# Moving the down-weight sums from the gate stage to the branch products, on GpSimd's queue

## The chip, the core and the metric

The kernel runs on one NeuronCore of a Trainium2 chip. The metric is the device time of one execution in microseconds. Engines are named as the profile names them: PE (TensorE), DVE (VectorE), ACT (ScalarE), POOL (GpSimd) and SP (SyncE), which here only issues DMAs.

## The reference

One layer of a streaming encoder on 1024 tokens of width 1024, all in float32. The input is normalized and projected; three mixers follow (latent attention "MLA", forgetting attention "fox", a Mamba-2 scan "SSD"), each with its own output weight; a sigmoid gate merges them; then comes a gated MLP with a causal convolution.

```
u = rms_norm(x, norm_mix_g) @ w_in              # u_mla, u_fox, u_ssm, u_gate
y_a, y_b, y_c = mla(u_mla) @ w_br_mla, fox(u_fox) @ w_br_fox, ssm(u_ssm) @ w_br_ssm
g = sigmoid(u_gate + b_gate)
x = x + (g0 * y_a + g1 * y_b + g2 * y_c) @ w_out
a = causal_dwconv(rms_norm(x, norm_ffn_g) @ ffn_w_up, ffn_conv_w, ffn_conv_b)
out = x + (silu(gate(a)) * val(a)) @ ffn_w_down
```

## The kernel before

Every large product is made of three float32r products (high by high, high by low, low by high), so an operand is first split: ACT copies the high part, DVE subtracts it for the low part (`split`, L133 and L134). A 128x512 product with eight blocks of the inner dimension is 24 matmuls.

The stages, in order:

- **Start (0 to about 92 us).** The tokens are normalized and the MLA input projections made. `columns` loads small constants as rows, transposes them on PE into columns (L292, L300) and copies them out on ACT. Its row tile `pr` has one buffer for three users: `pr_g`, and two `pr_f` of two DMAs each (L298).
- **MLA heads and fox values (to 206).**
- **fx (206 to 397).** Four weight blocks of 512 columns (`which` = 3, 0, 1, 4) times eight token tiles `t`, so 32 units, in a written-out order on PE, DVE and ACT. In each unit a few side jobs are placed. `split512` splits one quarter of the next block's weights. `gate_sums` is a generator of which one step runs per unit: the softplus terms, cumulative sums by matmuls with triangular matrices, the transposes `tp` of the fox sums in two halves with their split into `Fh` and `Fl`, then three matmuls into `pd`, their exponentials, a fourth matmul with `trim` into the same bank, and last the transpose of `cum`. `turned` transposes the queries or keys of an earlier unit into a `tp` bank (L699), of which there are two. `down_sums(k)` prepares a Strassen-like scheme for the last stage: from rows k and k+11 of the down weight it makes four 128x512 differences.
- **Attention (397 to about 895),** both kinds, with the conv and gate projections (`mm`, L860) as filling work on PE. GpSimd scales the softmax rows (`pm`, L977).
- **SSD scan (to about 1105),** with the rest of the filling work. PE, DVE and ACT follow a written-out order, planned with costs and due times.
- **Branch products (1119 to 1293).** For each branch b in the order fox (1), MLA (0), SSD (2) the input is loaded and split, and for each of eight output blocks j the weight block is loaded, the gate `gl` is loaded into one of the four `t4` buffers, two products `ybr` are made, DVE multiplies by the gate (L1326), and the sum is added to `mg`: on GpSimd for MLA (L1329), on DVE for SSD (L1331).
- **Output product, second norm, up projection (to 1824), down projection (to the end).** The down projection has seven steps of eleven blocks; steps P5, P6, P7 and P4 read the differences from the buffer `wsum_d` in device memory.

In fx `down_sums` uses the four shared `t4` buffers; SP issues two loads of 512 KB and two stores of 512 KB for each k, with the loads pinned to program order, and GpSimd makes four subtractions of 128x512.

Where no order is written out (SP and GpSimd everywhere, all engines in the branch products), the Tile framework chooses the order of each queue when the program is built. An engine then works through its queue in order; an instruction waits for what it reads and for its buffer.

Of the kernel before, what the change touches and what calls it, by code (L numbers as in the profile page):

```python
# [11 lines left out]
F32 = mybir.dt.float32  # L12
# [9 lines left out]
P = 128  # L22
# [12 lines left out]
NFH = NFF // 2  # L35
# [7 lines left out]
def block_kernel(ctx: ExitStack, tc: tile.TileContext, x, positions, norm_mix_g, w_in, b_gate,  # L43
# [5 lines left out]
    V, A, G, T, SY = nc.vector, nc.scalar, nc.gpsimd, nc.tensor, nc.sync  # L49
# [76 lines left out]
    def uid(s):  # L126
        cnt[0] += 1
        return f"{s}_{cnt[0]}"

    def split(h, l, src, he=None, le=None):  # L130
        he = he or A
        le = le or V
        i = A.activation(h, src, AF.Copy) if he is A else he.tensor_copy(h, src)  # L133
        return i, le.tensor_sub(l, src, f32(h))  # L134
# [27 lines left out]
    def alloc_hn():  # L162
        h = [hp.tile([P, NK, 512], F32R, name=uid("hnh"), tag=f"hnh{i}") for i in range(2)]
        l = [hp.tile([P, NK, 512], F32R, name=uid("hnl"), tag=f"hnl{i}") for i in range(2)]
        return h, l
# [118 lines left out]

    def columns(rp):

        pr = rp.tile([84, P], F32, name="pr_g", tag="pr", bufs=1)
        SY.dma_start(pr[0:24, :], b_gate.rearrange("o (r p) -> (o r) p", p=P))
        SY.dma_start(pr[24:72, :], ssm_conv_w.rearrange("o k (r p) -> (o k r) p", p=P))
        SY.dma_start(pr[72:84, :], ssm_conv_b.rearrange("o (r p) -> (o r) p", p=P))  # L290
        pt = psp.tile([P, 84], F32, name="pcp", tag="tp", bufs=2)
        T.transpose(pt, pr, ident[0:84, 0:84])  # L292
        A.activation(pc_g, pt, AF.Copy, scale=0.5)
        for dst, srcs in ((pc_f1, (ffn_conv_w[:, 0, :], ffn_conv_w[:, 1, :])),
                          (pc_f2, (ffn_conv_w[:, 2, :], ffn_conv_b))):
            pr = rp.tile([88, P], F32, name=uid("pr_f"), tag="pr", bufs=1)
            for i, s in enumerate(srcs):
                SY.dma_start(pr[44 * i:44 * i + 44, :], s.rearrange("o (r p) -> (o r) p", p=P))  # L298
            pt = psp.tile([P, 88], F32, name=uid("pcp"), tag="tp", bufs=2)
            T.transpose(pt, pr, ident[0:88, 0:88])  # L300
            A.activation(dst, pt, AF.Copy)
        pr = rp.tile([NK, P], F32, name="pr_n", tag="prn", bufs=1)
        SY.dma_start(pr, ssm_norm_g.rearrange("o (r p) -> (o r) p", p=P))
        pt = psp.tile([P, NK], F32, name="pcn", tag="tp", bufs=2)
        T.transpose(pt, pr, ident[0:NK, 0:NK])
        A.activation(pc_n, pt, AF.Copy)
        for col, src, sc in ((gq_col, mla_q_gain, 96.0 ** -0.5), (gk_col, mla_k_gain, 1.0)):
            V.memset(col, 1.0)
            SY.dma_start(col[0:64, :], src[0, 0:64].rearrange("(p o) -> p o", o=1))
            if sc != 1.0:  # L310
                V.tensor_scalar_mul(col, col, sc)
        for col, src, sc in ((fq_col, fox_q_gain, 0.125), (fk_col, fox_k_gain, 1.0)):
            SY.dma_start(col[0:64, :], src[0].rearrange("(p o) -> p o", o=1))
            SY.dma_start(col[64:128, :], src[0].rearrange("(p o) -> p o", o=1))
            if sc != 1.0:
                V.tensor_scalar_mul(col, col, sc)
# [282 lines left out]
    def gate_sums():  # L599
# [43 lines left out]
        for g in range(2):  # L643
            pt = tps([8, 4, P])
            for j in range(4):
                T.transpose(pt[:, j, :], F[:, 4 * g + j, :], ident)
            split(Fh[:, 512 * g:512 * g + 512], Fl[:, 512 * g:512 * g + 512], pt.rearrange("p j s -> p (j s)"))
        neg = fp.tile([8, P], F32, name="neg", tag="neg")
        V.memset(neg, -1.0)
        for r in range(4):  # L650
# [8 lines left out]
        T.matmul(pd[:, 0:128], tri, dv, start=True, stop=True)  # L659
        T.matmul(pd[:, 128:256], strict, dv, start=True, stop=True)  # L660
        T.matmul(pd[:, 256:384], ones, dv, start=True, stop=True)
        for i, dst in enumerate((ea, dend, cdec)):
            A.activation(dst.rearrange("p t h -> p (t h)"), pd[:, 128 * i:128 * i + 128], AF.Exp)
        V.tensor_mul(dend, dend, dt)

        T.matmul(pd[:, 384:512], trim, dv, start=True, stop=True)
        cum = ft("cum", (P, P))
        V.tensor_copy(cum, pd[:, 384:512])
        yield
# [6 lines left out]


    with px:
        def down_sums(k):

            w1, w2, s12, s34 = (fpl.tile([P, 2, 512], F32, name=uid("ws"), tag="t4", bufs=4) for _ in range(4))
            for w, r in ((w1, k), (w2, k + NFH)):
                tc.keep_in_program_order(SY.dma_start(
                    w, ffn_w_down[0, r * P:r * P + P, :].rearrange("p (b c) -> p b c", b=2)))
            G.tensor_sub(s12[:, 0, :], w1[:, 1, :], w1[:, 0, :])
            G.tensor_sub(s34[:, 0, :], w2[:, 1, :], w1[:, 1, :])
            G.tensor_sub(s12[:, 1, :], w2[:, 1, :], s12[:, 0, :])
            G.tensor_sub(s34[:, 1, :], w2[:, 0, :], s12[:, 1, :])
            SY.dma_start(wsum_d[k, :, 0:2, :], s12)
            SY.dma_start(wsum_d[k, :, 2:4, :], s34)  # L690

        units = 0
        gs = gate_sums()
        waiting = []
# [16 lines left out]
        with tc.manual_schedule(engines={mybir.EngineType.PE, mybir.EngineType.DVE, mybir.EngineType.Activation}):  # L711
            for i, which in enumerate((3, 0, 1, 4)):
                wh, wl = (lambda k, w=w5[i], j=j: w[k - k % 2][:, j, k % 2, :] for j in range(2))
                for t in range(NT):
                    if which != 4 and t == 0:
                        load512({3: C_FQ, 0: C_FQ + 512, 1: C_Z + 512}[which])
                    if which != 4 and t % 2:
                        split512()
                    if units % 5 in (1, 3) and units // 5 * 2 + units % 5 // 2 < NFH:
                        down_sums(units // 5 * 2 + units % 5 // 2)  # L720
                    p = acc("fx", "mv" if units % 3 == 2 else "mm")
                    units += 1
                    mm3(p, tok(hnh, t), tok(hnl, t), wh, wl, NK)
# [28 lines left out]
    def load_w(pool, src, nk=NK, he=None, le=None):  # L752
        raw = pool.tile([P, nk, P], F32, name=uid("wr"), tag="wr")
        SY.dma_start(raw, src)
        h = pool.tile([P, nk, P], F32R, name=uid("wh"), tag="wh")
        l = pool.tile([P, nk, P], F32R, name=uid("wl"), tag="wl")
        split(h, l, raw, he, le)
        return h, l
# [532 lines left out]
    with ExitStack() as pe_:  # L1291
# [5 lines left out]
            pass  # L1297
        run_until(clk[0] + 100.0)
        mh, ml = alloc_hn()
        for b, wsrc, nk in ((1, w_br_fox, 4), (0, w_br_mla, 4), (2, w_br_ssm, 8)):  # L1300
            ah, al = [], []
            for k in range(nk):
# [12 lines left out]
            wv = wsrc[0].rearrange("(k p) c -> p k c", p=P)  # L1315
            for j in range(NK):
                wh, wl = load_w(fpl, wv[:, :, j * P:j * P + P], nk)
                g = fpl.tile([P, S], F32, name=uid("gl"), tag="t4", bufs=4)
                SY.dma_start(g, g_d[b][j])
                for half in range(2):  # L1320
# [281 lines left out]
    for n, i in enumerate(turns, 1):  # L1602
# [41 lines left out]
        if not early:  # L1644
# [10 lines left out]
    wd = ffn_w_down[0].rearrange("(r p) c -> r p c", p=P)  # L1655
    steps = ("P1", "P2", "P5", "P6", "P3", "P7", "P4")
    wsrc = {"P1": lambda k: wd[k, :, 0:512], "P2": lambda k: wd[k + NFH, :, 0:512],
            "P5": lambda k: wsum_d[k, :, 0, :], "P6": lambda k: wsum_d[k, :, 1, :],
            "P3": lambda k: wd[k + NFH, :, 512:], "P7": lambda k: wsum_d[k, :, 2, :],
            "P4": lambda k: wsum_d[k, :, 3, :]}  # L1660

    def ablock(r, c, k):
        return act_d[k + NFH * c, :, 512 * r:512 * r + 512]
# [142 lines left out]
```

## Time and profile before

| | |
|---|---|
| three timed runs, median | 2041.64 us (2039.97 to 2042.64) |
| the profiled execution | 2035.85 us, its span 2034.1 us |
| granted PE clock, mean | 0.998 |
| busy: PE, DVE, ACT, POOL | 1988.9, 1411.8, 944.0, 615.4 us |
| loads `ws` of the down weight | 22 of 512 KB, on SP |
| stores to `wsum_d` | 22 of 512 KB, on SP |
| read from and written to device memory | 209.03 and 92.67 MB |

A row of waits has the engine and line, what it waited for, the total in us, how often, and the longest. A row of a timeline has the start and duration in us, the instruction, and in brackets the idle time before it with what ended it. A row of grouped instructions has, behind the bar, the busy time in us, the mean duration in ns and the idle time before them. A row of the table by windows has the stretch, its length, and then for each engine the busy us with the number of instructions, the granted PE clock, the DMA share and GB/s. Matmuls overlap in the pipeline, so starts, not durations, tell PE's pace.

### The profile page before, as it was taken

To read this page: it belongs to the slowest core of one execution; us is meant where nothing else is said; L and a number is where in the kernel's file an instruction comes from. 1 tells how busy PE (TensorE), PEld (TensorE's weight loads), DVE (VectorE), ACT (ScalarE), POOL (GpSimd) and SP (SyncE) were. 2 spreads that over 40 slices of the span, in tenths; PEclk is the share of its full clock that TensorE was granted. 3 is DMA by queue.
4 is the path that set the end of the run, shared out by engine and by line. 5 is a ranking of instruction groups with operands and counts; after the bars stand their busy time and mean duration, and the time that the engine had idled before them with its cause. 6 is when DMAs were issued, how large, how long until landed. Compare 5 with 4: busy or idle time off the path is not lost.

```text
span 2034.1 us, 28550 instructions
## 1 busy us (share of the span) xinstructions
PE 1988.9 (98%) x10041; PEld 1677.0 (82%) x10041; DVE 1411.8 (69%) x2628; ACT 944.0 (46%) x1722; POOL 615.4 (30%) x599
## 2 busy tenths in 40 slices
PE   7999999999999999999999999999999999999999
PEld 7899878888888888888778888888778888878887
DVE  7778589277768877856773455567997777775665
ACT  5555323166656666655553222224544444444432
POOL 4344233232222222210000040001565445412755
PEclk9999999999999999999999999999999999999999
DMA  5157877655535544434433663431322222239675
GB/s 170 46 182 263 290 227 230 201 141 141 133 100 134 139 125 117 114 115 140 129 113 126 229 219 114 158 122 52 93 94 81 85 83 83 84 122 335 210 239 190
DMA packets 277863, 303.58 MB, mean 149 GB/s; under 512 B 18860, under 2 KB 206520, under 8 KB 277720
## 3 DMA queue, kind: packets, MB, share of 16 engines
q1 hardware_dynamic: 276632, 299.66, 48.0%
q10 hardware_dynamic: 1088, 2.10, 0.3%
q8 instruction: 79, 1.29, 0.3%
q14 instruction: 64, 0.52, 0.1%
HBM read 209.03 MB, written 92.67 MB: 148 GB/s over the span
## 4 chain that ended last, share of the span: by engine, by line
PE 81%; DVE 10%; DMA 3%; ACT 2%; issue 2%; POOL 1%; SPq 1%; ACTq 0%; DVEq 0%; POOLq 0%
PE mm L860 18%; PE dn L1753 10%; PE ybr L158 9%; PE ua L1418 5%; PE uc L1418 5%; PE ud L1418 4%; PE fx L158 4%; PE wo L1464 4%; PE s L953 4%; PE tp L1023 3%; PE ub L1418 2%; PE fxv L158 1%; PE q L158 1%; PE py L1203 1%; PE o L1002 1%
## 5 line engine op out<-in xcount | busy, mean ns | idle before, releaser
L860 PE MATMUL mm<-hnh,wh 128*128 128x512 f32 x576 | 245.9, 427 | 0.0
L860 PE MATMUL mm<-hnh,wl 128*128 128x512 f32 x576 | 226.4, 393 | 0.0
L860 PE MATMUL mm<-hnl,wh 128*128 128x512 f32 x576 | 225.1, 391 | 0.0
L977 POOL TENSOR_SCALAR pm<-pm,rs 128x128 f32<-128x128 f32 (+7 forms) x128 | 113.1, 887 | 327.9 <-DVE rs L976 206.6
L1753 PE MATMUL dn<-dr,dr 128*128 128x512 f32 x592 | 182.3, 389 | 0.0
L158 PE MATMUL fx<-w,hnh 128*128 128x512 f32 x512 | 161.0, 395 | 1.8 <-DVE w L134 1.8
L1029 DVE TENSOR_TENSOR ptl<-tp,pth 128x512 fp32r<-128x512 f32 (+1 forms) x160 | 101.1, 632 | 46.6 <-ACT pth L1028 45.6
L1753 PEld LDWEIGHTS dn<-dr,dr 128*128 128x128 f32 x592 | 111.1, 188 | 23.1
L860 PEld LDWEIGHTS mm<-hnh,wl 128*128 128x128 f32 x576 | 108.1, 188 | 24.7
L970 ACT ACTIVATE pm<-s,nmx 128x128 f32<-128x128 f32 (+2 forms) x192 | 109.7, 577 | 38.7 <-DVE nmx L967 24.3
L1028 ACT ACTIVATE pth<-tp 128x512 fp32r<-128x512 f32 (+1 forms) x160 | 88.3, 553 | 78.1 <-PE tp L1023 77.4
L860 PEld LDWEIGHTS mm<-hnh,wh 128*128 128x128 f32 x576 | 108.6, 189 | 18.9 <-issue 5.0
L860 PEld LDWEIGHTS mm<-hnl,wh 128*128 128x128 f32 x576 | 109.0, 189 | 17.9 <-issue 3.1
L953 PE MATMUL s<-qk,qk 96*128 96x384 f32 (+5 forms) x480 | 116.3, 350 | 1.3 <-DMA qk<-q_l 0.9
L960 DVE TENSOR_REDUCE nmx<-s 128x1 f32<-128x128 f32 (+2 forms) x192 | 106.5, 555 | 13.7 <-PE s L953 9.2
L1329 POOL TENSOR_TENSOR mg<-mg,gl 128x512 f32<-128x512 f32 x16 | 24.8, 1559 | 299.8 <-DVE gl L1326 299.6
L1753 PE MATMUL dn<-dr 128*128 128x512 f32 x296 | 115.2, 389 | 0.0
L158 PEld LDWEIGHTS fx<-w,hnh 128*128 128x128 f32 x512 | 95.5, 189 | 21.5 <-DVE w L134 2.6
L134 DVE TENSOR_TENSOR dr<-dr,dr 128x1024 fp32r<-128x1024 f32 x52 | 72.7, 1398 | 54.5 <-ACT dr L133 53.9
L158 PE MATMUL fx<-w,hnl 128*128 128x512 f32 x256 | 100.2, 392 | 0.0
L158 PE MATMUL ybr<-al,wh 128*128 128x512 f32 x256 | 99.1, 389 | 0.0
L158 PE MATMUL ybr<-ah,wl 128*128 128x512 f32 x256 | 98.3, 389 | 0.0
(486 smaller groups left out, 5550.1 us busy)
## 6 DMA issues: line engine op xcount, KB each, us to landing
dr<-act_d SPq DMA_DIRECT2D x99, 256.0 KB
wr<-in_ffn_w_up_dram SPq DMA_DIRECT2D x47, 512.0 KB
wr<-in_w_in_dram SPq DMA_DIRECT2D x36, 512.0 KB
g_d<-t SPq DMA_DIRECT2D x24, 512.0 KB
gl<-g_d SPq DMA_DIRECT2D x24, 512.0 KB
ws<-in_ffn_w_down_dram SPq DMA_DIRECT2D x22, 512.0 KB
wsum_d<-ws SPq DMA_DIRECT2D x22, 512.0 KB
act_d<-fa SPq DMA_DIRECT2D x22, 512.0 KB
```

What stands on the lines that cost most here:

```text
L134: return i, le.tensor_sub(l, src, f32(h))
L158: T.matmul(ps, a(k), b(k), start=(i == 0), stop=(i == n - 1))
L860: T.matmul(ps, a[:, k, :], b[half][:, k, :], start=(k == 0 and i == 0), stop=(k == NK - 1 and i == 2))
L953: T.matmul(ps[:, :w], q_[:, qs], k_[:, a:a + w], start=i_ == 0, stop=i_ == len(o.passes) - 1)
L960: later(c + 0.101, lambda ps=ps, ci=ci, a=a, b=b: V.reduce_max(nmx[:, ci:ci + 1], ps[:, :b - a], axis=AX, negate=True))
L970: pss[ci][1][0] = later(c + 0.9 + 0.1 * ci, lambda ci=ci, a=a, b=b: A.activation(p_[:, a:b], pss[ci][0][:, :b - a], AF.Exp, bias=nb, accum ...
L977: G.tensor_scalar(p_[:, 0:n * P], p_[:, 0:n * P], rs[:, 3:4], 0.0, op0=ALU.mult, op1=ALU.add)
L1028: later(c + 0.05, lambda th=th, pt=pt, off=off: A.activation(th[:, :off], pt[:, :off], AF.Copy))
L1029: pl[0] = later(c + 0.6, lambda th=th, tl=tl, pt=pt, off=off: V.tensor_sub(tl[:, :off], pt[:, :off], f32(th[:, :off])))
L1418: T.matmul(ps, a, b, start=first and n == 0, stop=n == 11, skip_group_check=not first)
L1464: T.matmul(p, a, b, start=k == 0 and i == 0, stop=k == NK - 1 and i == 2)
L1753: T.matmul(ps[m], a[:, ts_], b[:, 512:], start=first_ and j == 0 and q == 0, stop=j == NFH - 1 and q == 2, skip_group_check=not first_)
```

## The change

- `pr` gets three buffers.
- `gate_sums` yields after each half of the fox transposes, so a half runs per unit and everything behind is two units later. The matmul with `trim` moves ahead of the three exponentials.
- `split512` runs at t = 1, 3, 5 and 6 of a block, instead of 1, 3, 5 and 7.
- `down_sums` leaves fx and runs in the loop over j of the branch products, before the gate is loaded: pieces of 128 columns, four for each k, 44 in all; two per j for fox, one per j for MLA, three or two per j for SSD. A piece uses one tile of 128x4x128 in a pool of the branch stage (three buffers), loads its two halves (2 x 128 KB), makes the four differences in place and stores them (256 KB), all in GpSimd's own queue. The order of the four differences in `wsum_d` changes, and with it the index that P6, P7 and P4 read.

```diff
-        pr = rp.tile([84, P], F32, name="pr_g", tag="pr", bufs=1)
+        pr = rp.tile([84, P], F32, name="pr_g", tag="pr", bufs=3)
...
-            pr = rp.tile([88, P], F32, name=uid("pr_f"), tag="pr", bufs=1)
+            pr = rp.tile([88, P], F32, name=uid("pr_f"), tag="pr", bufs=3)
...
             split(Fh[:, 512 * g:512 * g + 512], Fl[:, 512 * g:512 * g + 512], pt.rearrange("p j s -> p (j s)"))
+            yield
...
         T.matmul(pd[:, 256:384], ones, dv, start=True, stop=True)
+        T.matmul(pd[:, 384:512], trim, dv, start=True, stop=True)
         for i, dst in enumerate((ea, dend, cdec)):
             A.activation(dst.rearrange("p t h -> p (t h)"), pd[:, 128 * i:128 * i + 128], AF.Exp)
         V.tensor_mul(dend, dend, dt)
-
-        T.matmul(pd[:, 384:512], trim, dv, start=True, stop=True)
...
-        def down_sums(k):
-
-            w1, w2, s12, s34 = (fpl.tile([P, 2, 512], F32, name=uid("ws"), tag="t4", bufs=4) for _ in range(4))
-            for w, r in ((w1, k), (w2, k + NFH)):
-                tc.keep_in_program_order(SY.dma_start(
-                    w, ffn_w_down[0, r * P:r * P + P, :].rearrange("p (b c) -> p b c", b=2)))
-            G.tensor_sub(s12[:, 0, :], w1[:, 1, :], w1[:, 0, :])
-            G.tensor_sub(s34[:, 0, :], w2[:, 1, :], w1[:, 1, :])
-            G.tensor_sub(s12[:, 1, :], w2[:, 1, :], s12[:, 0, :])
-            G.tensor_sub(s34[:, 1, :], w2[:, 0, :], s12[:, 1, :])
-            SY.dma_start(wsum_d[k, :, 0:2, :], s12)
-            SY.dma_start(wsum_d[k, :, 2:4, :], s34)
...
-                    if which != 4 and t % 2:
+                    if which != 4 and t in (1, 3, 5, 6):
                         split512()
-                    if units % 5 in (1, 3) and units // 5 * 2 + units % 5 // 2 < NFH:
-                        down_sums(units // 5 * 2 + units % 5 // 2)
...
+        parts = [(k, c) for k in range(NFH) for c in range(0, 512, P)]
+
+        def down_sums():
+            k, c = parts.pop(0)
+            w = mp_.tile([P, 4, P], F32, name=uid("ws"), tag="ws", bufs=3)
+            for i, r in enumerate((k, k + NFH)):
+                G.dma_start(w[:, 2 * i:2 * i + 2, :],
+                            ffn_w_down[0, r * P:r * P + P, :].rearrange("p (b c) -> p b c", b=2)[:, :, c:c + P])
+            for o, i, j in ((0, 1, 0), (1, 3, 1), (3, 3, 0), (2, 2, 3)):
+                G.tensor_sub(w[:, o, :], w[:, i, :], w[:, j, :])
+            G.dma_start(wsum_d[k, :, :, c:c + P], w)
...
                 wh, wl = load_w(fpl, wv[:, :, j * P:j * P + P], nk)
+                for _ in range((1, 2, 3 - j % 2)[b]):
+                    if parts:
+                        down_sums()
```

More of the change, by code (lines that the diff above doesn't have):

```diff
@@ L1657, in block_kernel @@
     wsrc = {"P1": lambda k: wd[k, :, 0:512], "P2": lambda k: wd[k + NFH, :, 0:512],
-            "P5": lambda k: wsum_d[k, :, 0, :], "P6": lambda k: wsum_d[k, :, 1, :],
-            "P3": lambda k: wd[k + NFH, :, 512:], "P7": lambda k: wsum_d[k, :, 2, :],
-            "P4": lambda k: wsum_d[k, :, 3, :]}
+            "P5": lambda k: wsum_d[k, :, 0, :], "P6": lambda k: wsum_d[k, :, 3, :],
+            "P3": lambda k: wd[k + NFH, :, 512:], "P7": lambda k: wsum_d[k, :, 1, :],
+            "P4": lambda k: wsum_d[k, :, 2, :]}
     def ablock(r, c, k):
```

## Prediction

> **What bounds the kernel now.** I read the page first (share of the engines), then the waits of TensorE, then its timeline at the longest waits, then the queues that the change touches.
>
> ```profile
> span 2034.1 us, 28550 instructions
> PE 1988.9 (98%) x10041; PEld 1677.0 (82%) x10041; DVE 1411.8 (69%) x2628; ACT 944.0 (46%) x1722; POOL 615.4 (30%) x599
> ```
> ```profile
> PE tp L699 <- DVE Fl L134: 1.8, 1, 1.8
> PE fx L158 <- DVE w L134: 1.8, 2, 1.3
> PE pcp L300 <- DMA pr_f<-in_ffn_conv_b_dram: 1.7, 1, 1.7
> ...
> PE pd L666 <- ACT cdec L663: 0.7, 1, 0.7
> ```
>
> TensorE (PE) is busy for 1988.9 of 2034.1 us. No edit here removes a matmul, so an edit pays only where PE stands still or runs slowly. The four rows from tp to pd are what the edits aim at: 1.8 + 1.8 + 1.7 + 0.7 = 6.0 us. The window table shows where there is room:
>
> ```profile
> core 0: us, PE busy (x) PEld busy (x) DVE busy (x) ACT busy (x) POOL busy (x), PEclk, DMA share, GB/s
> 255.00:306.00 51.00, 48.46 (x229) 39.98 (x228) 44.72 (x132) 13.99 (x24) 15.70 (x12) 0.97 0.72 225
> 306.00:357.00 51.00, 49.72 (x235) 40.82 (x234) 47.76 (x135) 15.31 (x22) 17.32 (x12) 1.00 0.75 228
> 700.00:900.00 200.00, 194.91 (x1124) 167.02 (x1123) 150.21 (x366) 125.82 (x308) 52.41 (x57) 1.00 0.45 120
> 900.00:1105.00 205.00, 204.44 (x1065) 165.26 (x1064) 133.91 (x243) 101.57 (x170) 0.00 (x0) 1.00 0.41 125
> 1119.00:1163.00 44.00, 44.00 (x196) 36.45 (x195) 20.64 (x28) 11.17 (x15) 0.00 (x0) 1.00 0.66 216
> 1163.00:1207.00 44.00, 44.00 (x196) 36.45 (x195) 22.35 (x29) 9.11 (x12) 22.41 (x15) 1.00 0.62 192
> ```
>
> The fx stage (255 to 357) has PE idle for 51 - 48.46 + 51 - 49.72 = 3.8 us, with VectorE (DVE) nearly full and the clock at 0.97 in one stretch. The SSD stage (900 to 1105) and the branch products (from 1119) have no PE idle time worth naming, and GpSimd (POOL) does nothing in SSD.
>
> **Constants in three buffers.** One buffer for `pr` made SP hold back the second load until the first transpose had read it:
>
> ```profile
> SPq L298 <- PE pcp L292: 43.5, 1, 43.5
> ```
> ```profile
> 90.35 0.27 PE L300 MATMUL pcp<-ident,pr_f 88*128 88x88 f32 x1 [1.68 <-DMA pr_f<-in_ffn_conv_b_dram]
> ```
> ```profile
> 91.75 0.62 DVE L417 SCALAR_TENSOR_TENSOR cn<-cq,r,gcq 128x384 f32<-128x384 f32 x1 [0.33 <-PE tp L424]
> ```
> ```profile
> 230.46 0.33 SPq L689 DMA_DIRECT2D wsum_d<-ws  x1
> ```
>
> With three buffers the four loads go out early and the 1.68 us go. What is next after the transpose is DVE's `cn`, and its row says that it waited for PE, so it moves forward too. The four DMAs now stand on SP before some x loads: 4 x 0.33 us (an SP issue, the last row) = 1.3 us at worst. Value -1.7, ends -1.7 and +1.3.
>
> **Gate sums, one half per unit, and the fourth cumulative product before the exponentials.** Rows of PE in the fx stage:
>
> ```profile
> 268.88 0.49 PE L666 MATMUL pd<-dtA,trim 128*128 128x128 f32 x2 [0.70 <-ACT cdec L663]
> 271.20 1.12 PE L699 MATMUL tp<-ident,fqn 128*128 128x128 f32 x4 [1.83 <-DVE Fl L134]
> 271.97 1.20 PE L158 MATMUL fx<-w,hnh 128*128 128x512 f32 x2
> 272.97 0.63 PE L158 MATMUL fx<-w,hnl 128*128 128x512 f32 x1
> 273.40 1.05 PE L158 MATMUL fx<-w,hnh 128*128 128x512 f32 x2
> 274.25 0.51 PE L158 MATMUL fx<-w,hnl 128*128 128x512 f32 x1
> 274.60 0.62 PE L158 MATMUL fx<-w,hnh 128*128 128x512 f32 x2
> ...
> 278.69 0.60 PE L699 MATMUL tp<-ident,fqn 128*128 128x128 f32 x4
> 279.05 0.71 PE L158 MATMUL fx<-w,hnh 128*128 128x512 f32 x2
> ```
> ```profile
> 1119.08 174.08 PE ybr L158 x768
> ```
>
> The two gate halves take both `tp` banks in one unit, so the transposes of `turned` wait 1.83 us for a bank. After the stalls PE is slow: four transposes take 271.97 - 271.20 = 0.77 us against 279.05 - 278.69 = 0.36, and six matmuls take 274.60 - 271.97 = 2.63 us against 6 x 174.08/768 = 1.36. One half per unit leaves `turned` the other bank, and moving the `trim` product ahead of the exponentials, which read the same bank, removes the 0.70. No instruction is added. Sum 0.70 + 1.83 + 0.41 + 1.27 = 4.2 us; ends -2.5 (the slow matmuls stay) and -4.2. The gate sums end two units later; their first reader is the attention, the stage after this one. I take -4.2, because the slow matmuls follow the stall directly.
>
> **Last quarter split at t = 6.** The second wait for `w`:
>
> ```profile
> 356.07 0.50 PE L158 MATMUL fx<-w,hnh 128*128 128x512 f32 x1 [1.28 <-DVE w L134]
> ```
>
> The split moves one unit (about 6 us) ahead in DVE's order, and 1.28 us go. The other 0.5 us of that wait lie at the stage's start and stay. Ends -1.3 and 0.
>
> **Down-weight sums out of fx.** Removed there: 44 DMAs on SP, 44 GpSimd subtractions, and what they do to DVE. The first two rows below are DVE while they run (255 to 357), the next two the same instructions after them (357 to 396):
>
> ```profile
> L150 DVE SCALAR_TENSOR_TENSOR fr<-rs_t,fr 128x8 f32<-128x8 f32 x45 | 9.6, 214 | 1.5
> L140 DVE TENSOR_SCALAR fr<-rs_i 128x8 int32<-128x8 int32 x15 | 6.6, 438 | 0.5
> ```
> ```profile
> L150 DVE SCALAR_TENSOR_TENSOR fr<-rs_t,fr 128x8 f32<-128x8 f32 x3 | 0.5, 166 | 0.1
> L140 DVE TENSOR_SCALAR fr<-rs_i 128x8 int32<-128x8 int32 x1 | 0.2, 171 | 0.0
> ```
>
> DVE gains (45 x 48 ns + 15 x 267 ns = 6.2 us in these two alone), SP too, but PE was busy beside them, so this is worth 0 beyond the stalls already counted.
>
> **The sums at their new place.** Added: 44 pieces, each two loads, four subtractions of 128x128 and one store, all in GpSimd's queue: 176 subtractions and 132 DMA issues. The bytes stay: 44 x 512 KB = 23 MB.
>
> ```profile
> L227 POOL TENSOR_TENSOR rt<-rt,rt 128x128 f32<-128x128 f32 x20 | 9.2, 460 | 1.5
> ```
> ```profile
> 1168.44 4.41 POOL L1329 TENSOR_TENSOR mg<-mg,gl 128x512 f32<-128x512 f32 x3 [283.60 <-DVE gl L1326]
> 1174.28 1.67 POOL L1329 TENSOR_TENSOR mg<-mg,gl 128x512 f32<-128x512 f32 x1 [1.43 <-DVE gl L1326]
> 1177.00 1.29 POOL L1329 TENSOR_TENSOR mg<-mg,gl 128x512 f32<-128x512 f32 x1 [1.05 <-DVE gl L1326]
> ```
> ```profile
> 1288.20 0.34 SPq L110 DMA_DIRECT2D gff<-in_norm_ffn_g_dram  x1
> ```
>
> 176 x 0.46 = 81 us of subtractions. A DMA issued by GpSimd is not in this trace; call its price p. The low end is SP's 0.33 us (44 us in all). The high end is a GpSimd instruction that moves as many elements as a store, the 1.67 us of a 128x512 add (220 us). So the pieces hold GpSimd for 125 to 301 us; I take the middle, p = 1.0, 213 us. GpSimd stands empty for 283.60 us ahead of its first `mg` add. Its order is left to Tile, and a new stage's load does not wait for the old stage to end (`gff` goes out at 1288.20, the products run until 1119.08 + 174.08 = 1293.16), so I expect GpSimd to run the pieces ahead, during SSD. All 44 fit in the hole if p is under (283.6 - 81)/132 = 1.53 us. The Trainium skill (DMA: Bandwidth & Descriptors, "Latency and other measured facts") gives about 1 us to the first byte on GpSimd's path, for descriptors written in software; by that the pieces would take 132 + 81 = 213 us as well and the sum would be the same; no run here shows it.
>
> Queued behind a piece that waits for its load are only later pieces and the sixteen adds; the sums' reader is the down projection, the last stage. The cost is DVE, held up by the subtractions, while PE's order in SSD is fixed. The nearest row with both engines loaded is 700 to 900: GpSimd 52 us, DVE 150, and PE loses 5.1 in 200 us. SSD with 81 us of short subtractions lies below that, since its DVE has 71 us idle. Value +1, ends 0 (nothing there gets shorter) and +5. DMA has the room: 0.41 of the time carries 125 GB/s, so 23 MB take some 76 us of the 205.
>
> **Sum.** -1.7 - 4.2 - 1.3 + 0 + 1 = -6.2 us. The profiled execution took 2035.85 us (span 2034.1), so 2029.6 like for like; the three timed runs have a median of 2041.64, so I predict 2035.4. Best corner: -1.7 - 4.2 - 1.3 = -7.2, 2034.4; worst: +1.3 - 2.5 + 0 + 5 = +3.8, 2045.4. A measurement of this kernel tells about 0.2%, 4.1 us, from no change.
>
> **Rivals.**
> GpSimd falls behind in the branch products (slower). If the pieces do not run ahead, the fox products give two per block of 5.44 us (two adds 1174.28 to 1177.00 are half a block) and the MLA products one beside two adds, with 1.43 + 1.05 = 2.48 us free. At p = 1.0 a piece takes 1.84 + 3.0 = 4.84 us: the lag grows by (9.68 - 5.44) x 8 = 34 us, then by (4.84 - 2.48) x 8 = 19, together 53. The adds hold the `gl` buffers; four of them give about three blocks, 16 us, before PE stands. Cost 37 us, 2041.6 - 7.2 + 37 = 2071. It decides (+4.1 net) once the lag passes 16 + 7.2 + 4.1 = 27 us. For it: the pieces stand in that loop. Against: the 283.60 us. Chance 0.13.
>
> DVE in SSD is held up more than its slack (+5 to +8 there): 2039 to 2043, no change. For: 133.91 us of DVE work there that each subtraction can hold up. Against: 71 us idle. Chance 0.14.
>
> The stalls only move, since DVE's chain of small operations ends next in fx: -2 at most, 2039.6, no change. For: DVE 47.76 of 51. Against: part of that load goes with the subtractions. Chance 0.11.
>
> DVE shuts GpSimd out (slower).
>
> ```profile
> L1161 DVE TENSOR_TENSOR xdt<-xT,dt 128x1024 f32<-128x1024 f32 x8 | 9.8, 1220 | 8.4 <-ACT xT L1152 8.4
> ```
>
> If each issue waits for one long DVE operation such as this, p is 1.67 + 1.22 = 2.9 us, the pieces take 81 + 383 = 464 us, 180 more than the hole, and even half of it ahead of the adds gives 90 - 16 = 74 us, near 2108. Against: SSD's DVE operations are tensor-tensor, not copies. Chance 0.05. The Trainium skill (SBUF — State Buffer, "SBUF: two separate sides") has this rule: while DVE runs a two-port operation GpSimd cannot write its descriptors. No run here shows it.
>
> **How the numbers follow.** Forecast 0.57, own range 2031 to 2040 (runs scatter by 2.7 us); no-change rivals 0.25; slower 0.18. I predict 2035.4; the range 2030 to 2048 leaves out the two slower rivals and covers the worst corner. Faster 0.57, same 0.24, slower 0.19 (a little of the SSD case ends past 4.1 us).
>
> **What would show it.** Right: no wait of tp for `Fl`, of pd for `cdec`, of pcp for a DMA; PE clock 1.00 over 255 to 306; small DVE operations in fx at 166 to 171 ns; GpSimd subtractions from about 1168 - 284 = 885 on; PE still full from 1119 to 1293. Wrong: GpSimd's last `mg` add well after the MLA block (1207), PE waiting for `gl` or `ah` there; PE waits for DVE in SSD; a new wait of fx matmuls.

## The result and the profile after

The change makes the kernel slower. The timed runs have a median of 2096.24 us (2091.8 to 2099.0, four runs) against 2040.81 us for the kernel before in the same session; the ratio is 1.0271, 95% interval 1.0255 to 1.0286. The forecast was 2035.4 us. The page of the changed kernel's profiled execution (2096.22 us):

```profile
span 2094.5 us, 28793 instructions
PE 1994.7 (95%) x10041; PEld 1683.2 (80%) x10041; DVE 1397.6 (67%) x2628; ACT 942.7 (45%) x1722; POOL 737.9 (35%) x863
```

PE is busy about as long as before (1988.9 us) in a span that is 60.4 us longer, so PE stands still. Its waits (total, times, longest) say where:

```profile
PE pt L1373 <- DVE xn L1365: 55.9, 1, 55.9
...
PE cq L158 <- DVE rs_i L139: 2.0, 1, 2.0
```

One wait holds nearly the whole loss: the transposes of the first second-norm (L1373, in the output stage) wait for `xn`, which DVE makes from ACT's sum of squares (L1360). The timeline of ACT, first of the kernel before, then of the changed one, in the same stage:

```profile
1303.47 1.06 ACT L133 ACTIVATE woh<-raw 128x1024 fp32r<-128x1024 f32 x1 [0.23 <-DMA raw<-in_w_out_dram]
1308.31 1.06 ACT L133 ACTIVATE wh<-wr 128x1024 fp32r<-128x1024 f32 x1 [3.78 <-DMA wr<-in_ffn_w_up_dram]
1315.72 1.06 ACT L1360 ACTIVATE xn<-x 128x1024 f32<-128x1024 f32 x1 [6.35 <-DVE x L1485]
```
```profile
1305.54 1.06 ACT L133 ACTIVATE woh<-raw 128x1024 fp32r<-128x1024 f32 x1 [0.33 <-DMA raw<-in_w_out_dram]
1367.98 1.06 ACT L133 ACTIVATE wh<-wr 128x1024 fp32r<-128x1024 f32 x1 [61.38 <-DMA wsum_d<-ws]
1370.99 1.06 ACT L1360 ACTIVATE xn<-x 128x1024 f32<-128x1024 f32 x1 [1.95 <-DVE x L1485]
```

The order on ACT is the same. Between the output weight and the norm stands the split of one up-projection block into `wh`. Before, it waited for its own weights (`wr`); now it waits 61.38 us for a store of `ws`, with which it has no data in common. What it shares, by the account tested below, is the place in SBUF (the core's on-chip memory): this `wh` is the third up-projection buffer (`whl()`, every third turn, pool `fill3`, opened once the branch pools are closed), and the `ws` buffers, allocated after `al`, lie on its strip. It may be written only when the last store from there has left, and ACT's later work waits behind it. GpSimd's timeline says why that store is late:

```profile
940.38 4.10 POOL L1294 TENSOR_TENSOR ws<-ws 128x128 f32<-128x128 f32 x4
1167.22 1.29 POOL L1329 TENSOR_TENSOR mg<-mg,gl 128x512 f32<-128x512 f32 x1 [222.74 <-DVE gl L1326]
...
1363.86 2.17 POOL L1295 DMA_DIRECT2D wsum_d<-ws  x3
```

The pieces do start in the hole (the first load is issued at 881.1), but after 11 of them the first `mg` add stands in the queue and waits for the branch product until 1167. The other 33 run behind it, among the adds and after, until 1366. A piece makes four subtractions; these are the ones ahead of the add (870 to 1167):

```profile
L1294 POOL TENSOR_TENSOR ws<-ws 128x128 f32<-128x128 f32 x44 | 26.4, 625 | 6.7 <-DMA ws<-in_ffn_w_down_dram 6.3
```

Some expectations below count 13 or 14 pieces at 4.6 us; the trace has 11 in those 63 us, about 5.8 us each.

Windows of the changed kernel, to be read against the prediction's table (PE, PEld, DVE, ACT, POOL busy, then PE clock):

```profile
255.00:306.00 51.00, 51.00 (x249) 42.44 (x248) 38.95 (x147) 13.77 (x24) 0.00 (x0) 1.00 0.43 113
306.00:357.00 51.00, 51.00 (x244) 42.18 (x243) 41.30 (x137) 16.27 (x24) 0.00 (x0) 1.00 0.42 106
900.00:1105.00 205.00, 203.15 (x1057) 163.89 (x1055) 135.94 (x241) 100.33 (x168) 34.77 (x52) 1.00 0.47 144
1207.00:1300.00 93.00, 93.00 (x411) 77.03 (x411) 59.37 (x72) 28.67 (x38) 69.30 (x103) 1.00 0.73 239
1300.00:1400.00 100.00, 44.07 (x195) 36.46 (x195) 23.64 (x58) 11.75 (x18) 54.20 (x100) 0.71 0.49 149
```

fx is full now and at clock 1.00; SSD loses 1.3 us (203.15 against 204.44); the branch products stay full, but for one wait of 0.8 us for `al`, beside GpSimd's work; the output stage loses 56.

The stages of all kernels, in us, from the first and last starts of their PE tiles: end of `cq`; first `fx` product; fx stage (first `fx` to first `mm`); SSD (first to last `seg`); output stage (first `wo` to first `ua`). Each row's stages are from one traced execution. The medians are from several sessions, and each ratio is to the kernel before in the same session.

| kernel | cq end | fx start | fx | SSD | output | median | ratio to before |
|---|---|---|---|---|---|---|---|
| before | 86.9 | 205.2 | 191.2 | 160.0 | 93.5 | | |
| after | 89.0 | 208.1 | 184.9 | 160.1 | 152.0 | 2096.24 | 1.0271 |
| e1_no_move | 89.0 | 208.7 | 191.3 | 160.0 | 93.5 | 2041.72 | 1.0013 |
| e1_move_only | 86.9 | 207.8 | 186.0 | 160.1 | 152.3 | 2094.88 | 1.0270 |
| e1_all_ahead | 88.1 | 206.9 | 185.0 | 160.1 | 159.4 | 2099.95 | 1.0295 |
| e1_late_split | 88.1 | 206.8 | 185.0 | 160.2 | 100.7 | 2044.65 | 1.0033 |
| e2_ahead | 88.8 | 206.5 | 185.0 | 161.0 | 93.4 | 2055.56 | 1.0076 |
| e2_fx_no_subs | 85.9 | 207.3 | 186.0 | 160.1 | 93.4 | 2034.35 | 0.9977 |
| e3_dve_adds | 89.1 | 207.5 | 186.6 | 164.9 | 97.8 | 2043.68 | 1.0015 |
| e3_dve_adds_pr1 | 86.3 | 206.4 | 185.0 | 167.1 | 97.6 | 2044.79 | 1.0030 |
| e3_no_edits | 86.7 | 209.6 | 186.0 | 168.3 | 95.9 | 2045.06 | 1.0025 |
| e4_no_subs | 89.1 | 208.9 | 185.0 | 160.1 | 93.4 | 2034.62 | 0.9974 |
| e4_place | 86.1 | 209.4 | 184.9 | 160.1 | 102.1 | 2045.57 | 1.0029 |
| e5_dve_subs | 86.9 | 206.5 | 185.0 | 160.1 | 107.0 | 2055.54 | 1.0080 |

### The profile page after: what moved, and what is told of

Read it like the earlier page. It is cut to its first block, busy times and chain, and to the rows that moved or that the text cites. A ratio compares the mean times of both kernels' runs of the same rounds, so it can differ in the third digit from the quotient of the medians.

```text
span 2094.5 us, 28793 instructions
## 1 busy us (share of the span) xinstructions
PE 1994.7 (95%) x10041; PEld 1683.2 (80%) x10041; DVE 1397.6 (67%) x2628; ACT 942.7 (45%) x1722; POOL 737.9 (35%) x863
## 5 line engine op out<-in xcount | busy, mean ns | idle before, releaser
L962 POOL TENSOR_SCALAR pm<-pm,rs 128x128 f32<-128x128 f32 (+7 forms) x128 | 113.1, 886 | 327.6 <-DVE rs L961 186.0
L133 ACT ACTIVATE wh<-wr 128x1024 fp32r<-128x1024 f32 (+1 forms) x47 | 43.0, 914 | 160.0 <-DMA wsum_d<-ws 61.4
L1294 POOL TENSOR_TENSOR ws<-ws 128x128 f32<-128x128 f32 x176 | 96.1, 574 | 22.6 <-DMA ws<-in_ffn_w_down_dram 22.0
```

Source lines behind the costliest of these rows:

```text
L962: G.tensor_scalar(p_[:, 0:n * P], p_[:, 0:n * P], rs[:, 3:4], 0.0, op0=ALU.mult, op1=ALU.add)
L1294: G.tensor_sub(w[:, o, :], w[:, i, :], w[:, j, :])
```

## Experiments

The theory to be tested ("S"): a strip of SBUF that changes hands ties two stages together, and an in-order queue spreads the wait. Its rivals: the small edits (E), GpSimd's backlog by itself (Q), and GpSimd slowing the other engines (D).

### Which part of the change it is

In the cuts of code below, ` ...` stands for lines left out. e1_no_move puts the old `down_sums` and its calls back into the changed kernel; e1_move_only is the kernel before with the new ones.

```diff
+                    if units % 5 in (1, 3) and units // 5 * 2 + units % 5 // 2 < NFH:
+                        down_sums(units // 5 * 2 + units % 5 // 2)
                     p = acc("fx", "mv" if units % 3 == 2 else "mm")
 ...
-                for _ in range((1, 2, 3 - j % 2)[b]):
-                    if parts:
-                        down_sums()
```

> The changed kernel with the down-weight sums put back into the fx stage (512 KB loads on SP's queue, as before); the three small edits stay. Theory S (the loss is the strip of the `ws` buffers, which the third up-projection weight buffer takes over: its first write waits on ScalarE until the last sum is stored): the 55.9 us wait of the norm's transposes is gone, the time is 2036 to 2041 (fx shorter by some 5, the start longer by 2.9). Rival E (the small edits cause the loss): still above 2080.

> The kernel before with the new place of the down-weight sums alone; constants, gate sums and last quarter as before. Theory S: the wait of the norm's transposes is there, 50 to 60 us, and the time is 2095 to 2102. Rival E: within 5 us of the kernel before.

The move alone gives the whole loss (1.0270, interval 1.0252 to 1.0287), with the same wait, and E is out:

```profile
PE pt L1373 <- DVE xn L1365: 56.1, 1, 56.1
```

Without the move the kernel is 0.13% slower (1.0003 to 1.0023), and fx is not shorter: 191.3 us. So the expectation's "shorter by some 5" was wrong. The named waits of the kernel before are gone there, but others stand in their place, and DVE's small operations are slower still, 293 ns against 214 in the kernel before (a wait of PE for DVE in fx, and a group of DVE's operations from 255 to 357):

```profile
PE tp L699 <- DVE fqn L745: 3.5, 2, 1.9
```
```profile
L150 DVE SCALAR_TENSOR_TENSOR fr<-rs_t,fr 128x8 f32<-128x8 f32 x42 | 12.3, 293 | 1.4
```

The move alone, with the old gate sums, makes fx 5.2 us shorter. What shortens fx is that the sums leave it.

### The queue: the same work, one split later

```diff
-            first[n] = halves(raw) if n < 3 else raw
+            first[n] = halves(raw) if n in (1, 2) else raw
 ...
     for n in FORDER[:3]:
+        if n == 0:
+            first[0] = tuple(whl())
+            tc.keep_in_program_order(split(*first[0], r0[0])[0])
         p1(n)
```

> The changed kernel with one split moved: the split of the up-projection block that uses the third weight buffer comes after the second norm's activations in ScalarE's and VectorE's queues, just before its product, instead of ahead of the first norm. GpSimd's work, its order, its transfers and the buffers' addresses stay; the last store still leaves near 1366. Theory S with the in-order queue: the norms no longer stand behind that split, so the wait of the transposes falls from 55.9 us to under 8 (GpSimd's own two subtractions of the norm, due at 1366 in the kernel before, are just in time), the time is 2038 to 2050. Rival Q (GpSimd's backlog holds up TensorE by itself, through its adds or the norm's subtractions): 2080 or more.

Measured 2044.65 us, 1.0033 (1.0021 to 1.0046). ACT now takes the norms first:

```profile
1313.53 1.06 ACT L1360 ACTIVATE xn<-x 128x1024 f32<-128x1024 f32 x1 [8.35 <-DVE x L1485]
```
```profile
1397.38 1.05 ACT L133 ACTIVATE wh<-wr 128x1024 fp32r<-128x1024 f32 x1
```
```profile
PE pt L1373 <- DVE xn L1365: 6.2, 2, 5.1
```

GpSimd's backlog is no shorter (its last store goes out at 1376.9, in the changed kernel at 1365.2), and 50 of the 55.9 us are gone. So the backlog is not what costs (Q is out); the split that waited for it at the head of ACT's and DVE's queues is.

### The strip: the same pieces at other addresses

e1_all_ahead issues all pieces ahead of the branch loop, and so allocates `ws` ahead of `ah` and `al`:

```diff
+        while parts:
+            down_sums()
+
         for b, wsrc, nk in ((1, w_br_fox, 4), (0, w_br_mla, 4), (2, w_br_ssm, 8)):
 ...
-                for _ in range((1, 2, 3 - j % 2)[b]):
-                    if parts:
-                        down_sums()
```

> The changed kernel with all 44 pieces issued ahead of the loop over the branches, so that they stand ahead of the first `mg` add in GpSimd's queue. In the changed kernel the first 13 or 14 pieces took 63 us from 881, 4.6 us each; 44 would end near 881 + 44 x 4.6 = 1083 to 1090, ahead of that add (1167) and far ahead of the third weight buffer (1308). Theory S: the wait of 55.9 us is gone; the SSD stage pays for three times as many subtractions (1.9 us of PE idle there with 14 pieces, against 0.6 before), +2 to +5; the time is 2036 to 2045. Rival D (GpSimd's transfers and subtractions slow the other engines wherever they lie): 2060 to 2090.

A miss, 2099.95 us, and the most telling one. GpSimd's first piece, ACT and PE's waits:

```profile
1076.63 4.56 POOL L1291 DMA_DIRECT2D ws<-in_ffn_w_down_dram  x6 [196.41 <-PE py L1188]
```
```profile
1363.34 2.00 ACT L133 ACTIVATE woh<-raw 128x1024 fp32r<-128x1024 f32 x2 [70.96 <-DMA wsum_d<-ws]
```
```profile
PE wo L1464 <- ACT woh L133: 59.1, 2, 57.9
```

By S, the new addresses were in use until the last `py` product of SSD (it starts at 1076.0), so the first piece began 196 us later, and their next owner is `woh`, the first weight of the output stage, so that it is now `woh` that waits for the last store. Where the buffer lies sets when the work can start and who waits for its end.

e2_ahead keeps the addresses (all pieces issued after the first branch's `ah` and `al`) and holds the adds behind them:

```diff
-                        G.tensor_add(m, m, g[:, hs])
+                        tc.keep_in_program_order(G.tensor_add(m, m, g[:, hs]))
```

> The changed kernel with all 44 pieces issued in the first branch, after its `ah` and `al` tiles are allocated (so that the `ws` buffers keep the addresses they have in the changed kernel), and the `mg` adds held to program order on GpSimd, behind the pieces. Theory S in its fuller form (a piece can start when the strip's last user has read it and blocks the strip's next user until its store has left; the changed kernel's strip is free from 881): the pieces run from 881 to about 881 + 44 x 4.6 = 1083, in the SSD stage, the third weight buffer waits for nothing, and the wait of 55.9 us is gone. The SSD stage lost 204.44 - 203.15 = 1.3 us of PE time to 14 pieces, so some 4 us to 44; the time is 2036 to 2042. Rival D (GpSimd's transfers and subtractions slow VectorE wherever they lie): PE idle in SSD grows by 10 us or more, 2046 or more.

The pieces run from 880 to 1133, the wait of 55.9 us is gone, and SSD takes 161.0 us, as S has it (the traced execution, at 2051.52 us, is the fastest of six). SSD's window:

```profile
900.00:1105.00 205.00, 203.05 (x1054) 163.52 (x1053) 144.15 (x241) 100.49 (x169) 162.34 (x251) 1.00 0.71 216
```

The time is 2055.56 us all the same, 1.0076 (1.0061 to 1.0091): the framework's order on SP came out differently too, and weight loads now stand ahead of the `gl` loads; SP spends 19.71 us on five of them, the `gl` loads come after, and PE waits for DVE's `gl`:

```profile
1163.71 19.71 SPq L739 DMA_DIRECT2D wr<-in_w_br_mla_dram  x5
```
```profile
PE ybr L158 <- DVE gl L1325: 9.1, 1, 9.1
```

In e2_ahead_pr1 and e3_dve_adds_pr1 `pr` is back in one buffer:

```diff
-        pr = rp.tile([84, P], F32, name="pr_g", tag="pr", bufs=3)
+        pr = rp.tile([84, P], F32, name="pr_g", tag="pr", bufs=1)
 ...
-            pr = rp.tile([88, P], F32, name=uid("pr_f"), tag="pr", bufs=3)
+            pr = rp.tile([88, P], F32, name=uid("pr_f"), tag="pr", bufs=1)
```

> The same with the constants back in one buffer. If the three buffers cost the start (last `cq` product at 88.1 to 89.0 in the runs with three, 86.9 in those with one), the last `cq` product is back at 86.9 and the time is 1 to 2 us below that of the run with three buffers; if they gain 1.7 us as the prediction had it, 1.7 us above.

For e2_ahead_pr1 only the time is used: 2055.7 us (1.0077), no difference from 2055.56.

### The order on GpSimd: adds on VectorE

```diff
-                        G.tensor_add(m, m, g[:, hs])
+                        V.tensor_add(m, m, g[:, hs])
```

> The changed kernel with one word changed: the sixteen `mg` adds of the MLA products run on VectorE (which has 22 of 44 us idle there) and no longer on GpSimd, so that nothing in GpSimd's queue stands among the pieces. Addresses, places of the pieces and the split of the third weight buffer as in the changed kernel. Theory S: the 30 pieces that stood behind the first add now run ahead too, from 881 to about 1130 (the run with all pieces ahead took 253 us for them); the wait of the norm's transposes is gone, SSD loses 1.4 us of PE time (205 - 203.05 against 205 - 204.44, as in that run), the time is 2032 to 2040. If the addresses alone make ScalarE wait, whatever the order in GpSimd's queue, it stays above 2085. Rival D (GpSimd holds up VectorE in SSD): 2045 or more.

> The same with the constants back in one buffer. Last `cq` product at 86 to 87 in place of 88 to 89; the first fx product follows 0 to 2 us earlier; 0 to 2 us faster than with three buffers. By the prediction's term it would be 1.7 us slower.

> The kernel before with the move of the sums and the adds on VectorE, without any of the three small edits. In the runs so far the fx stage took 186.0 us with the move alone and 184.8 to 185.0 with the edits too: by that the gate sums and the earlier split are worth 1.1 us once the subtractions are gone, and this kernel is 1 us slower than the one with constants in one buffer and the edits, and still 1 to 5 us faster than the kernel before. If the two edits are worth what the prediction had (4.2 + 1.3), it is 5.5 us slower than that kernel.

With nothing in GpSimd's queue to wait for, all pieces are done by 1140 and the wait of 55.9 us is gone from all three: one word undoes nearly all of the loss of 2.7%. But they are not faster than the kernel before, and miss the 2032 to 2040 that S gave: 1.0015 (1.0005 to 1.0025), 1.0030 (1.0014 to 1.0045), 1.0025 (1.0015 to 1.0035). The fx stage keeps its 5 us, and SSD gives 5 to 8 back. SSD's window of e3_dve_adds, and DVE in it (905 to 1105), first of the kernel before, then of e3_dve_adds:

```profile
900.00:1105.00 205.00, 199.21 (x1033) 159.89 (x1032) 151.08 (x241) 99.07 (x166) 165.26 (x257) 1.00 0.71 217
```
```profile
L1186 DVE TENSOR_TENSOR E<-E,cbm 128x512 f32<-128x512 f32 x32 | 22.1, 691 | 23.3 <-ACT E L1185 23.1
L1246 DVE SCALAR_TENSOR_TENSOR y<-y,t 128x1024 f32<-128x1024 f32 x8 | 9.8, 1219 | 0.0
L1163 DVE TENSOR_TENSOR xdd<-xT,dend 128x1024 f32<-128x1024 f32 x8 | 9.7, 1218 | 0.0
L1232 DVE TENSOR_TENSOR hst<-hst,ts 128x512 f32<-128x512 f32 x12 | 8.3, 688 | 4.4 <-PE ts L1226 3.8
```
```profile
L1171 DVE TENSOR_TENSOR E<-E,cbm 128x512 f32<-128x512 f32 x32 | 24.8, 778 | 18.8 <-ACT E L1170 18.7
L1231 DVE SCALAR_TENSOR_TENSOR y<-y,t 128x1024 f32<-128x1024 f32 x8 | 15.1, 1884 | 0.0
L1148 DVE TENSOR_TENSOR xdd<-xT,dend 128x1024 f32<-128x1024 f32 x8 | 12.4, 1547 | 0.0
L1217 DVE TENSOR_TENSOR hst<-hst,ts 128x512 f32<-128x512 f32 x12 | 8.3, 689 | 2.7 <-PE ts L1211 1.9
```

The same instructions take longer, up to 1884 ns for 1219, where both operands lie in SBUF; the one that reads `ts`, a PSUM tile, is untouched (689 for 688). The e3 kernels pay 5 to 8 us where e2_ahead, with the same 44 pieces at the same addresses, paid 1.0 in its one trace; why is open.

### The price of the subtractions

Twice the subtractions are left out, and the loaded weights stored in place of the sums, so that DMAs and bytes stay: in fx of the kernel before, and in e3_dve_adds.

```diff
-            G.tensor_sub(s12[:, 0, :], w1[:, 1, :], w1[:, 0, :])
-            G.tensor_sub(s34[:, 0, :], w2[:, 1, :], w1[:, 1, :])
-            G.tensor_sub(s12[:, 1, :], w2[:, 1, :], s12[:, 0, :])
-            G.tensor_sub(s34[:, 1, :], w2[:, 0, :], s12[:, 1, :])
-            SY.dma_start(wsum_d[k, :, 0:2, :], s12)
-            SY.dma_start(wsum_d[k, :, 2:4, :], s34)
+            SY.dma_start(wsum_d[k, :, 0:2, :], w1)
+            SY.dma_start(wsum_d[k, :, 2:4, :], w2)
```

> The kernel before with the 44 x 4 subtractions of the fx stage left out: the loads on SP stay, and the loaded weights are stored in place of the sums, so that the bytes stay too. The fx stage takes 191.2 us in the kernel before (205.2 to 396.4), 191.3 with the three small edits alone and 186.0 with the move alone. If GpSimd's subtractions hold up VectorE there, the stage takes 184 to 187 us and the small VectorE operations fall from 214 to about 166 ns; if SP's queue or the transfers do it, 190 to 192 us with 214 ns.

```diff
-            for o, i, j in ((0, 1, 0), (1, 3, 1), (3, 3, 0), (2, 2, 3)):
-                G.tensor_sub(w[:, o, :], w[:, i, :], w[:, j, :])
```

> The kernel with the adds on VectorE (the move, the three edits), with the 176 subtractions left out: GpSimd still issues all 132 DMAs, and the loaded weights are stored in place of the sums. With the subtractions the SSD stage's products took 164.9 to 168.3 us from first to last (`seg`), VectorE was busy 150 to 151 of 205 us, against 160.0 and 134 in the kernel before. If the subtractions hold up VectorE (as in fx, where leaving them out gave the 5 us), SSD is back at 160 to 161 with VectorE at 134 to 136, and the time is 2032 to 2036. If GpSimd's DMAs or their traffic do it, it stays at 164 or more and 2040 or more.

Both came out as the first alternative has it: 0.9977 (0.9967 to 0.9988) and 0.9974 (0.9964 to 0.9985). fx falls to 186.0 us with the old gate sums and the old place of the last split, and DVE's operations there fall to:

```profile
L150 DVE SCALAR_TENSOR_TENSOR fr<-rs_t,fr 128x8 f32<-128x8 f32 x48 | 8.0, 167 | 1.6
L140 DVE TENSOR_SCALAR fr<-rs_i 128x8 int32<-128x8 int32 x16 | 2.8, 172 | 0.5
```

And SSD of e4_no_subs, with all of GpSimd's DMAs in it, is as full as in the kernel before, with DVE at 133.45 us:

```profile
900.00:1105.00 205.00, 204.44 (x1065) 165.22 (x1063) 133.45 (x241) 101.12 (x169) 82.99 (x116) 1.00 0.74 227
```

So DMAs and traffic cost nothing here, at 227 GB/s. GpSimd's arithmetic beside DVE's costs about 5 us in fx, and in SSD between 1.0 (e2_ahead) and 8.3 us (e3_no_edits). These two kernels, which lack the sums, mark what a free place would give: some 4 us.

### Two tries at a free place

e4_place puts `ws` on the strip that lies between SSD's `yT` and the second norm's `T3f`, by alternating `ah` and `al` in buffers of their own and allocating `ws` after the seventh pair:

```diff
-                h = mp_.tile([P, S], F32R, name=uid("ah"), tag="ah", bufs=8)
-                l = mp_.tile([P, S], F32R, name=uid("al"), tag="al", bufs=8)
+                h = mp_.tile([P, S], F32R, name=uid("ah"), tag=f"ah{slot[0] % 8}", bufs=1)
+                l = mp_.tile([P, S], F32R, name=uid("al"), tag=f"al{slot[0] % 8}", bufs=1)
+                slot[0] += 1
+                while slot[0] == 7 and parts:
+                    down_sums()
```

> The kernel with the adds on VectorE and one buffer for the constants, with another strip for the `ws` buffers: they lie where the SSD stage's `yT` lay and where the second norm's `T3f` will lie, and the `ah` and `al` buffers alternate to leave that place. Theory S: the pieces can start only when the last `yT` has been stored, near 1107, and block nobody until `T3f` is first written, near 1363; 44 pieces of 4.5 to 5.2 us end between 1305 and 1340. So SSD is as short as in the kernel before (160 us), fx keeps its 5 us, TensorE stays full over the branch products, and the norms in the output stage wait at most 3 us for VectorE: 2032 to 2038, the fastest so far. If theory S is wrong about what starts the pieces, they begin near 881 again and SSD takes 165 or more.

The first piece starts when S says, set by the owner that S names:

```profile
1108.12 4.55 POOL L1291 DMA_DIRECT2D ws<-in_ffn_w_down_dram  x6 [225.62 <-DMA ys_d<-yT]
```
```profile
PE pt L1374 <- DVE xn L1366: 5.7, 2, 3.5
```
```profile
1376.52 0.69 DVE L1383 TENSOR_TENSOR T3f<-pt,b 128x512 f32<-128x512 f32 x1 [5.11 <-DMA wsum_d<-ws]
```

SSD and fx are as short as expected, but the output stage takes 102.1 us, and the time is 2045.57 us, 1.0029 (1.0014 to 1.0044). The pieces last until 1372, past the first write of `T3f`, so DVE waits 5.11 us there for the last store, and a norm behind it comes late: the failure of the changed kernel again, on a smaller scale. The longer of PE's two waits, 3.5 us at the first norm, is the one that the e3 kernels have too (see the end of this section).

e5_dve_subs makes the subtractions on DVE, spread over the branch products (the adds on DVE and `pr` in one buffer, as in e3_dve_adds_pr1):

```diff
-                G.tensor_sub(w[:, o, :], w[:, i, :], w[:, j, :])
+                V.tensor_sub(w[:, o, :], w[:, i, :], w[:, j, :])
 ...
+            while b == 1 and len(parts) > 36:
+                down_sums()
 ...
-                for _ in range((1, 2, 3 - j % 2)[b]):
+                for _ in range((1, 1, 3 - j % 2)[b]):
```

> The kernel with the adds on VectorE and one buffer for the constants; the 176 subtractions of the pieces too run on VectorE, GpSimd only issues the DMAs; eight pieces stand ahead of the fox products, one goes with each fox and MLA block, two or three with each SSM block. VectorE is held to the program's order in SSD, so the subtractions lie in the branch products, where it was busy 101 of 195 us (23.78 + 22.35 + 54.52). At 200 to 280 ns each (the 128x128 product `cbm` took 281 to 284 ns in SSD) they add 35 to 49 us there. If the price of the sums is that GpSimd and VectorE work at the same time, it is gone wherever they lie: SSD 160 us, fx 185 us, the output stage 92.4 us, and the time is that of the kernels without subtractions, 2032 to 2037. If it is the work as such (VectorE late for TensorE because of it), the branch products grow from 174 us to 178 or more, 2038 or more.

SSD and fx are short and DVE's own operations keep their length, but DVE's in-order queue now waits for the pieces' loads, and the low half of an output weight (`wol`) comes late. 2055.54 us, 1.0080 (1.0068 to 1.0093). The waits of DVE (1060 to 1320) and of PE:

```profile
DVE ws L1294 <- DMA ws<-in_ffn_w_down_dram: 38.2, 23, 4.5
```
```profile
PE wo L1466 <- DVE wol L134: 8.4, 1, 8.4
```

The question put to it, whether the price goes when the two engines don't work at once, is not answered by its time. No version that makes the sums beat the kernel before.

The output stages of the e3 kernels, 95.9 to 97.8 us, are 2 to 4 us longer than before although their pieces are long done. Their DVE queue has another order: two splits of the output weight (`wol`) stand behind three adds `x` that wait for PE. The load of the up-projection block waits for those splits, up to 7.9 us on SP against 2.3 before, so the `wh` split that stands ahead of the first norm waits 8.51 us for its weights against 3.78, and PE stands still for 2.5 to 2.6 us at the norm. DVE and ACT of e3_dve_adds, to be read against ACT's rows of the kernel before in the section on the result:

```profile
1315.47 2.35 DVE L134 TENSOR_TENSOR wol<-raw,woh 128x1024 fp32r<-128x1024 f32 x2
```
```profile
1320.86 1.06 ACT L133 ACTIVATE wh<-wr 128x1024 fp32r<-128x1024 f32 x1 [8.51 <-DMA wr<-in_ffn_w_up_dram]
```

In the kernel before these two splits ran from 1303.27 on. e4_no_subs has the adds on DVE too, but the old order and an output stage of 93.4 us. Why the framework chose the other order is not known.

## Why the prediction was wrong, step by step

**The step that failed** is in "The sums at their new place": "Queued behind a piece that waits for its load are only later pieces and the sixteen adds; the sums' reader is the down projection, the last stage." The reader of the data was looked for, the next owner of the buffer was not. That owner, the third up-projection weight buffer, stands at the head of ACT's queue ahead of the norms: a wait of 55.9 us, in a term that the sum had at +1. The same step had all 44 pieces run ahead, although the order was left to the framework; the order it chose lets 11 by and then waits 222.74 us for an add. It took both to make the loss: e3_dve_adds undoes the order, e1_late_split the queue on ACT, and either takes away most of it. The forecast's condition, p under 1.53, was met and did not help.

**The price of an issue**, taken as 1.0 us, and the subtractions, taken as 0.46 us, in the changed kernel (busy, mean ns, idle before):

```profile
L1294 POOL TENSOR_TENSOR ws<-ws 128x128 f32<-128x128 f32 x176 | 96.1, 574 | 22.6 <-DMA ws<-in_ffn_w_down_dram 22.0
L1291 POOL DMA_DIRECT2D ws<-in_ffn_w_down_dram x88 | 63.0, 720 | 24.7 <-DMA wsum_d<-ws 22.5 <-issue 2.0
L1295 POOL DMA_DIRECT2D wsum_d<-ws x44 | 32.5, 762 | 0.7 <-POOL ws L1294 0.6
```

An issue holds the queue for 0.72 to 0.76 us, inside the bounds. That is not the time to the data: from issue to landing a load takes 4.4 us (last section), so a time to the first byte was the wrong thing to set beside p. The subtractions take 0.57 us on average. The pieces take 191.6 us busy and 48 in waits, nearly all for their own loads and stores, which the sum of 213 did not have; run ahead without a break they take 253 us (e2_ahead, 880 to 1133), which still fits the hole.

**DVE in SSD**, +1: the size came out in the changed kernel (1.3 us of PE idle more), but by luck: only 11 pieces lie there, PE's one new wait of that size, 1.3 us, is for a DMA (`bc`), and the stage from first to last `seg` is no longer than before (160.1 us). With all pieces in SSD it is right for e2_ahead (161.0 for 160.0) and too small for the three e3 kernels, 5 to 8. So had the pieces run ahead as forecast, the rival "DVE in SSD is held up more than its slack" may well have come true; the runs don't decide it.

**Gate sums, the fourth product and the last quarter**, -4.2 and -1.3, with the sums' leaving at 0: the total came near (-5.5 forecast; fx 191.2 to 184.9, -6.3) by luck, with the attribution reversed. The edits without the move give 0 (191.3), the move without the edits -5.2 (186.0), and leaving out the subtractions alone takes away the waits for `Fl` and for the second `w` too. The edits add about 1 us: fx takes 185.0 with the move and all edits, and the 0.7 us wait for `cdec` goes with them alone. In time, e3_no_edits and e3_dve_adds_pr1 are 0.3 us apart, not the 5.5 of the sum. The waits that the prediction summed were symptoms of a DVE slowed by GpSimd, and its own rows (214 against 166 ns, 438 against 171) said so; "PE was busy beside them" was the wrong reason to put them at 0. The rival that the stalls only move is what e1_no_move shows.

**Constants in three buffers**, -1.7: the wait for `pr_f` went as said, but `cq` ends at 88.1 to 89.1 us with three buffers and at 85.9 to 86.9 with one, with a new wait of 2.0 us for `rs_i`. The first fx product comes at 206.5 to 208.9 and 205.2 to 209.6, so nothing is left of it either way.

**The rivals.** `gl` as the way to the loss did not come about: the last `mg` add of the MLA block ran at 1208.6 as before, and PE was full from 1207 to 1300. Of DVE shutting GpSimd out of its descriptors nothing is seen: an issue took 0.68 to 0.94 us in the changed kernel, beside DVE's SSD and branch work (a single one of 2.26 us stands in e4_no_subs).

**What was to show it.** The waits of tp for `Fl`, of pd for `cdec` and of pcp for a DMA are gone, the clock over 255 to 306 is 1.00, DVE's small operations in fx take 167 to 172 ns, the subtractions begin at 885.9 and PE is full over the branch products but for 0.8 us: every sign of being right came true, and the loss came where no sign had been named, in the stage after.

## What to carry to other kernels

When an operation is moved, ask of each buffer it takes: who owned this strip before, who owns it next, and what stands in that owner's in-order queue behind its first write; the reader of the data is only half of the question. Where a framework chooses the order of a queue, look the order up in a trace before counting on it; here the choice made the loss, and changed the order on SP and DVE in later versions. Before costing edits that each remove a stall, look whether the stalls have one cause: instructions of the same shape that take longer in that stage than elsewhere point to it. Work that slows a neighbour by sharing something with it is not made free by moving it beside the same neighbour.

## What the runs showed of the hardware

GpSimd's arithmetic and DVE's lengthen each other, and by operand: in SSD beside the pieces (e3_dve_adds), DVE operations with both operands in SBUF rose from 691 to 778, 1218 to 1547 and 1219 to 1884 ns, the one with a PSUM operand stayed at 688 to 689, and GpSimd's 128x128 subtraction, 460 to 468 ns in the median, has a mean of 566 to 647 in the kernels with the move. The Trainium skill (SBUF — State Buffer, "SBUF: two separate sides") has a rule that fits: DVE and GpSimd share a pair of SBUF ports that one instruction holds for its whole length, and a DVE operation with two SBUF inputs takes it against a GpSimd operation that reads SBUF. Without GpSimd's arithmetic, 116 of its DMA issues in the 205 us of SSD's window left DVE at 133.45 us, against 133.91 before.

Over 1300 to 1400 of the changed kernel, in which PE stood still for 56 us, the granted clock was 0.71 with 44.07 us of work done; in the kernel before it was 1.00 there, with PE full. A load or store of the pieces, from issue to landing (median in us, last column):

```profile
ws<-in_ffn_w_down_dram POOLq DMA_DIRECT2D x88, 128.0 KB, 4.4
wsum_d<-ws POOLq DMA_DIRECT2D x44, 256.0 KB, 3.4
```
